# SSD decays without TensorE: broadcast rows in two buffers each, loaded a chunk ahead, and five steps of the backward states per chunk

## The chip, the cores and the metric

The kernel runs on one core of one Trainium2 chip. The metric is the device time of one execution in microseconds (us), as the median of several runs. A core has five engines that work side by side, each through its own instructions in order: TensorE (PE in the profile; PEld is its weight load), VectorE (DVE), ScalarE (ACT), GpSimd (POOL) and SyncE (SP), which here issues nearly all of the DMA transfers.

## What is computed

A two-layer backbone over 1024 latent positions and 256 context positions with 1024 features: one layer of windowed attention, then one layer with a bidirectional Mamba-2 mixer (SSD). The change lies in the second layer. Its scan is computed in chunks of 128 positions; the reference, cut to what matters here:

```python
a_cs = jnp.cumsum(da, axis=2)                      # within a chunk, per head
decay_to_end = jnp.exp(a_last[:, :, None] - a_cs)
states = jnp.einsum('bcsgn,bcsgr,bcsgrp->bcgrpn', bm, decay_to_end, xdt)
...
diff = a_cs[:, :, :, None] - a_cs[:, :, None, :]
lmat = jnp.exp(jnp.where(lower, diff, -jnp.inf))
cb = jnp.einsum('bcqgn,bcsgn->bcqsg', cm, bm)
y_diag = jnp.einsum('bcqsg,bcqsgr,bcsgrp->bcqgrp', cb, lmat, xdt)
y_off = jnp.einsum('bcqgn,bcgrpn,bcqgr->bcqgrp', cm, h_prev, jnp.exp(a_cs))
y = (y_diag + y_off)
```

This is done once forward and once on the reversed sequence, and the two results are added. There are 8 groups of 4 heads, 64 features a head, and 128 state entries.

## The kernel before, in words

The time up to about 780 us goes to the attention layer, which the change does not touch. Then `ssd_consts` (L778) computes, for all 64 rows (32 heads, two directions) and all positions, the step sizes dt, their logarithm ln, the sums acs of dt times A within each chunk (forward for rows 0 to 31, backward for 32 to 63), and from them tables with the positions on the partitions: `dtdec`, `eacs` and `dtb`, each transposed on TensorE (L885 to L889) and copied out by ScalarE (L886 to L891). Two halves of the positions go through this one after the other (L830).

The scan (`ssd`, L1025) then goes through 8 groups with 8 chunks each, 64 slots in all (`slot`, L1122). In a slot, M is a matrix of 128 x 4 x 128: for four heads, the factor between position k (partition) and position q (column). For q after k it is the forward decay times dt, otherwise the backward one, so that one M serves both directions. M times the product of B and C (`pcb`, L1130, L1134) is then the weight of four matmuls with x (L1159), which give the part of y within the chunk. L1132 and L1133 give the parts from the states before and after the chunk; L1139 and L1140 move the forward state on. The rest of a slot adds the skip term, multiplies by the gate, normalizes (L1167 to L1175) and stores the transposed result as `uN` one slot later (`tail`, L1187 to L1189).

How M comes about before the change: the sums acs and the values ln - acs are each split by `rows` (L855) into a rounded part and a remainder, and written to DRAM. For each chunk three small loads bring 20 rows into `rraw` (L1105, L1107), whose rest holds constants 0 and 1; ScalarE rounds them into `rrow` for TensorE (L1110). One matmul with `rrow` as weights and as moving operand adds a row value acs[q] and a partition value ln[k] - acs[k]. `decays` (L1114) does this for half of the heads at a time, two matmuls for the two directions (L1118), then a predicated copy takes the backward one where q is before k (L1119, mask `before`), and ScalarE applies the exponential and writes M (L1120). The first half of M for the next chunk is computed about the middle of a slot (L1166), the second half a little later (L1174).

Between these steps, `fill` lets the projections of the next group run (`front`, L911; in the last group the output projection `ssd_out`, L1261). They give TensorE most of its work: matmuls of 512 columns (L984) and 256 columns (L975, L1009), three for each product, since each operand is split into a rounded part and a remainder. Weights are loaded a use ahead (L920), rounded by ScalarE (L924) and their remainder taken by VectorE (L928).

The backward states of the next group form a chain of 11 steps (`states`, L1069): GpSimd weights x (L1059, two buffers) and decays the state before (L1064), TensorE multiplies with B into one PSUM buffer (L1082), and VectorE adds (L1094). `tick` (L1238) takes one step of this chain; a slot calls it three times at its end, as soon as the next group's x is there. What is left of the chain is issued at the end of the group (L1253).

This is the order in which the program issues instructions. A list scheduler with a model of the engines then orders them for each engine, and tile pools put in the waits where a buffer is reused. The order on each engine is thus fixed when the kernel is built. PSUM has three buffers `psX` for the small products of a slot, one `psD` and two `pj2`.

Of the kernel before, what the change touches and what calls it, by code (L numbers as in the profile page):

```python
# [9 lines left out]
F32 = mybir.dt.float32  # L10
# [3 lines left out]
ALU = mybir.AluOpType  # L14
# [30 lines left out]
    oraw=3, h1=2, h1k=8, wada=8, sqa=1,  # L45
    cacc=2, cctx=1, bT=2, cT=2, xn4=4, xn2=1, bn4=4, bn2=1, sz=2, xw=2, hf=2, hx=2, M=2, y2=1, xs=1, uT=2, pj2=2, psX=3, sk=2, dg=2,
)
# [60 lines left out]
class Kernel:  # L108
# [669 lines left out]
    def ssd_consts(self, p):  # L778
# [14 lines left out]
        self.half = t(p, [P, 1], F32, "half")  # L793
        nc.vector.memset(self.half, -0.5)
        self.eacs = t(p, [P, NCH, 64], F32, "eacs")
        self.dtdec = t(p, [P, NT, 64], F32, "dtdec")
        self.dtb = t(p, [P, NCH, 32], F32, "dtb")
        self.eal = t(p, [P, 64, NT], F32, "eal")

        self.acs_d = t(dr, [2, 64, LAT], F32, "acs")  # L800
        self.v_d = t(dr, [2, 64, LAT], F32, "vrow")
        self.before = t(p, [P, P], mybir.dt.int32, "before")
# [27 lines left out]
        for lo, n, chunks in ((0, 768, (0, 1, 2, 3, 8, 9)), (768, 512, (4, 5, 6, 7))):  # L830
# [23 lines left out]
            nc.vector.tensor_tensor_scan(out=acs[32:, ::-1], data0=keep[32:, :n][:, ::-1], data1=da[32:, ::-1], initial=0.0, op0=ALU.mult, op1=ALU.add)  # L854
            def rows(dst, src):  # L855
                h = t(q, [64, 512], F32R, "rowh", 2)
                l = t(q, [64, 512], F32R, "rowl", 2)
                nc.scalar.copy(h, src[:, :512])
                nc.vector.tensor_sub(l, src[:, :512], h)
                for x, y in enumerate((h, l)):  # L860
                    nc.sync.dma_start(dst[x, :, chunks[0] * P : chunks[0] * P + 512], y.bitcast(F32))

            rows(self.acs_d, acs)
            av = acs.rearrange("p (c n) -> p c n", n=P)
# [9 lines left out]
            nc.vector.tensor_sub(ln, ln, acs)  # L874
            rows(self.v_d, ln)

# [3 lines left out]
            nc.vector.tensor_mul(dd, dd, dt)  # L880
            nc.scalar.activation(acs, acs, AF.Exp)
            for b, c in enumerate(chunks):
                sl = slice(b * P, (b + 1) * P)
                pt = t(ps, [P, 256], F32, "psX")
                nc.tensor.transpose(pt[:, 0:64], dd[:, sl], self.ident[:64, :64])  # L885
                nc.scalar.copy(self.dtdec[:, c, :], pt[:, 0:64])  # L886
                if c < NCH:
                    nc.tensor.transpose(pt[:, 64:128], acs[:, sl], self.ident[:64, :64])
                    nc.tensor.transpose(pt[:, 128:192], dt[:, sl], self.ident[:64, :64])  # L889
                    nc.scalar.copy(self.eacs[:, c, :], pt[:, 64:128])  # L890
                    nc.scalar.copy(self.dtb[:, c, :], pt[:, 160:192])  # L891
        nc.sync.dma_start(self.eal, eal_d.broadcast_to([P, 64, NT]))

# [131 lines left out]
    def ssd(self, c0):  # L1025
# [8 lines left out]
        ps2 = self.pool("scan", ctx=c0)  # L1034


        rraw = t(ps2, [32, 6, P], F32, "rraw")
        rrow = t(ps2, [P, 6, P], F32R, "rrow")
        nc.sync.dma_start(rraw, a["rrow"].rearrange("p (r n) -> p r n", r=6))
        nc.vector.memset(rrow.bitcast(F32), 0.0)  # L1040
        ys = []
# [6 lines left out]
        def hd(d, g):  # L1048
            return slice(32 * d + 4 * g, 32 * d + 4 * g + 4)
# [19 lines left out]
        def states(g, st):  # L1069

            st["hb"] = {}
            jobs = [(0, 8), (0, 9), (1, 9), (1, 8)] + [(1, c) for c in range(NCH - 1, 0, -1)]
            xw = {}
            h = None
            for n, (d, c) in enumerate(jobs):
                if n == 0:
                    xw[0] = xweight(st, g, c, d)
                    yield
                if n + 1 < len(jobs):
                    xw[n + 1] = xweight(st, g, jobs[n + 1][1], jobs[n + 1][0])  # L1080
                s = t(ps, [P, 512], F32, "psD")[:, :256]
                nc.tensor.matmul(s, B(st, c), flat(xw.pop(n)), start=True, stop=True)  # L1082
                sv = s.rearrange("p (r h) -> p r h", r=R)
                if n in (0, 2):
                    h = t(ps2, [P, R, HP], F32, "hx")
                    nc.scalar.copy(h, sv)
                else:
                    if n == 1:
                        hn = t(ps2, [P, R, HP], F32, "hf0")
                    else:  # L1090
                        o = NCH - 1 if n == 3 else c - 1
                        hn = t(ps2, [P, R, HP], F32, f"hb{o if g % 2 == 0 else NCH - 1 - o}")
                    decay(hn, h, g, c, d)
                    nc.vector.tensor_add(hn, hn, sv)  # L1094
                    if n == 1:
                        st["hf"] = hn
                    else:
                        st["hb"][o] = h = hn
                yield

        def load_rows(n):
            g, c = divmod(n, NCH)
            cs = slice(c * P, (c + 1) * P)
            ar = self.acs_d.rearrange("h (d k) n -> (h d) k n", d=2)[:, 4 * g : 4 * g + 4, cs]
            nc.sync.dma_start(rraw[0:4, :4], ar)  # L1105
            for d in range(2):
                nc.sync.dma_start(rraw[4 + 8 * d : 12 + 8 * d, 4 + d], self.v_d[:, hd(d, g), cs])  # L1107

        def round_rows(n):
            nc.scalar.copy(rrow[:32], rraw)  # L1110
            if n + 1 < G * NCH:
                load_rows(n + 1)

        def decays(n, M, half):  # L1114

            o = t(ps, [P, 512], F32, "psX").rearrange("p (d r n) -> p d r n", d=2, r=2)
            for d in range(2):
                nc.tensor.matmul(o[:, d], rrow[:, 4 + d], rrow[:, 2 * half : 2 * half + 2], start=True, stop=True)  # L1118
            nc.vector.copy_predicated(o[:, 0], self.before.unsqueeze(1).broadcast_to([P, 2, P]), o[:, 1])  # L1119
            nc.scalar.activation(M[:, 2 * half : 2 * half + 2], o[:, 0], AF.Exp)  # L1120

        def slot(n, st, M, fill, tick, last):  # L1122

            g, c = divmod(n, NCH)
            cs = slice(c * P, (c + 1) * P)
            xc = X(st, c).rearrange("p (r h) -> p r h", r=R)
            if n + 1 < G * NCH:
                round_rows(n + 1)
            pcb = t(ps, [P, 512], F32, "psX")[:, :P]
# [5 lines left out]
            if c < NCH - 1:  # L1135
# [55 lines left out]
            self.tail = tail  # L1191
            return nM

        post = Queue()
        st = {}
        load_rows(0)
        done = 0.0
# [11 lines left out]
        for _ in chain:  # L1209
            pass  # L1210
        M = t(ps2, [P, R, P], F32, "M")
        round_rows(0)
        for half in range(2):
            decays(0, M, half)
        st["xw"] = xweight(st, 0, 0, 0)
        self.tail = None
        with ExitStack():
            for g in range(G):
# [25 lines left out]
                for c in range(NCH):  # L1244
                    def fill(x):
                        run(total * (c + sum(SEGS[: x + 1]) / sum(SEGS)) / NCH)
                    M = slot(g * NCH + c, st, M, fill, tick, g == G - 1)
                if g < G - 1:
                    run(1e9)
                    while 1 not in nst or not nst["sz"]:  # L1250
                        post.pop()
                    chain = chain or states(g + 1, nst)
                    for _ in chain:  # L1253
                        pass
                    nst["xw"] = xweight(nst, g + 1, 0, 0)
                    st = nst
# [223 lines left out]
def layout(i):  # L1480
# [26 lines left out]
    z = np.zeros((P, P), np.float32)  # L1507

    rr = np.zeros((32, 6, P), np.float32)
    for x in range(4):  # L1510
        for r in range(R):
            rr[4 + 4 * x + r, r] = 1.0
        rr[x, 4 + x % 2] = 1.0
    d["rrow"] = rr.reshape(32, -1)
    d["mask"] = np.concatenate([lm, z, rm, z, z, lm, z, z, z], 1).astype(np.float32)
# [29 lines left out]
```

## Time and profile before

| | |
|---|---|
| median of 3 runs | 1880.89 us (1879.43 to 1883.35) |
| profiled execution | 1880.79 us |
| its span, first to last instruction | 1878.7 us |
| mean granted TensorE clock | 0.980 |
| matmuls on PE | 10,632 instructions |
| DMA traffic | 192.10 MB in 147,203 packets |

Of a row that groups instructions, the name before the arrow is the tile written and those behind it are the tiles read. Three numbers with slashes are the shortest, the median and the longest duration in ns. In a row by window stand the window, its length, the busy time of each engine with its number of instructions, then the granted TensorE clock, the share of the DMA engines' time and GB/s. In a row in order of time stand start, duration, engine, line, operation and tiles; "x2" at the end means two instructions in one row, and brackets name how long the engine was idle ahead of it and whom it waited for.

### The profile page before, as it was taken

The page shows a single profiled execution, that of the slowest core. Times are in us where ns is not written, and L with a number is a line of the kernel's source. Part 1 is how long each engine was busy: PE and PEld are TensorE (multiplying, and loading weights), DVE is VectorE, ACT ScalarE, POOL GpSimd, SP SyncE. Part 2 cuts the span into 40 slices and gives each one's busy share as a digit, 9 for nine tenths or more (in the row PEclk, how much of TensorE's full clock was granted, in tenths as well). Part 3 has the DMA queues.
Part 4 walks back from the last instruction along what each step waited for, and adds up shares of the span by engine and source line. Part 5 has one row for each costly group of instructions (what it writes and reads, how often), then busy time and mean ns, then how long its engine had stood idle before and what let it go on. Part 6 is the DMA issues. An engine that isn't in the chain of part 4 may idle for free. (4 is left out here: it accounts for less than half of the span.)

```text
span 1878.7 us, 29635 instructions
## 1 busy us (share of the span) xinstructions
PE 1790.6 (95%) x10632; PEld 1541.9 (82%) x10632; DVE 1178.2 (63%) x2199; ACT 906.5 (48%) x1861; POOL 758.8 (40%) x1029
## 2 busy tenths in 40 slices
PE   6899998899999899979999999999999999999997
PEld 2687776788888786668898898989889898988887
DVE  3754426887777766584665758666575766754843
ACT  4522326677778665562353535434353544543632
POOL 4741107654456454302343343524335252442411
PEclk8899999999999999989999999999999999999998
DMA  9348756553345446111111111111111111433552
GB/s 357 108 118 260 240 167 157 126 126 95 97 120 134 113 129 222 59 56 34 38 36 44 47 33 44 39 41 36 44 47 33 47 38 39 141 117 100 177 153 78
DMA packets 147203, 192.10 MB, mean 102 GB/s; under 512 B 15312, under 2 KB 84816, under 8 KB 147056
## 3 DMA queue, kind: packets, MB, share of 16 engines
q1 hardware_dynamic: 112992, 171.56, 29.0%
q0 software_dynamic: 34064, 18.65, 5.5%
q8 instruction: 84, 1.38, 0.3%
q14 instruction: 63, 0.52, 0.1%
HBM read 154.54 MB, written 35.92 MB: 101 GB/s over the span
## 5 line engine op out<-in xcount | busy, mean ns | idle before, releaser
L229 PE MATMUL pj<-uH,wh 128*128 128x512 f32 (+1 forms) x712 | 259.3, 365 | 12.1 <-DVE v L542 2.8
L230 PE MATMUL pj<-uL,wh 128*128 128x512 f32 (+1 forms) x712 | 245.1, 345 | 1.3 <-DVE uL L298 0.9
L231 PE MATMUL pj<-uH,wl 128*128 128x512 f32 (+1 forms) x712 | 244.5, 344 | 1.1 <-POOL wl L217 1.1
L1059 POOL TENSOR_TENSOR xw<-xn,dtdec 128x256 f32<-128x256 f32 x144 | 105.9, 738 | 206.6 <-PE psD L1082 102.1
L984 PE MATMUL pj<-uH,wh 128*128 128x512 f32 x512 | 171.7, 405 | 1.1 <-ACT xn L951 1.1
L984 PE MATMUL pj<-uH,wl 128*128 128x512 f32 x512 | 171.8, 405 | 0.0
L229 PEld LDWEIGHTS pj<-uH,wh 128*128 128x128 f32 x712 | 136.7, 192 | 40.5 <-issue 11.9
L984 PE MATMUL pj<-uL,wh 128*128 128x512 f32 x512 | 168.3, 399 | 0.0
L217 POOL TENSOR_TENSOR wl<-wr,wh 128x512 fp32r<-128x512 f32 x96 | 127.2, 1329 | 77.7 <-ACT wh L215 67.1
L631 DVE TENSOR_TENSOR pl<-pt,ph 128x512 fp32r<-128x512 f32 x168 | 114.5, 687 | 64.6 <-ACT ph L630 63.5
L1009 PE MATMUL pj<-wh,uH 128*128 128x256 f32 x512 | 154.7, 302 | 0.0
L1009 PE MATMUL pj<-wh,uL 128*128 128x256 f32 x512 | 151.3, 295 | 0.0
L231 PEld LDWEIGHTS pj<-uH,wl 128*128 128x128 f32 x712 | 136.4, 192 | 17.7 <-POOL wl L217 1.5
L1009 PE MATMUL pj<-wl,uH 128*128 128x256 f32 x512 | 150.8, 295 | 0.0
L230 PEld LDWEIGHTS pj<-uL,wh 128*128 128x128 f32 x712 | 136.9, 192 | 14.0 <-DVE uL L298 1.4
L215 ACT CAST wh<-wr 128x512 fp32r<-128x512 f32 (+1 forms) x136 | 87.3, 643 | 116.8 <-PE pj L230 75.2
L1188 ACT ACTIVATE uT<-psX,nw 128x128 f32<-128x128 f32 x128 | 47.0, 367 | 189.9 <-PE psX L1187 188.8
L605 DVE CUSTOM_DVE_ANT_0 sm<-S,mask,nsink 128x640 f32<-128x640 f32 (+2 forms) x160 | 119.1, 772 | 26.7 <-PE S L602 13.8
L630 ACT CAST ph<-pt 128x512 fp32r<-128x512 f32 x168 | 97.6, 586 | 61.8 <-PE pt L626 56.2
L607 ACT ACTIVATE sm<-sm,nm 128x640 f32<-128x640 f32 (+2 forms) x160 | 118.5, 742 | 9.5 <-DVE nm L605 9.0
L1154 POOL TENSOR_TENSOR xs<-xn,sk 128x256 f32<-128x256 f32 x64 | 42.0, 657 | 184.8 <-DVE sk L1150 183.6
L984 PEld LDWEIGHTS pj<-uL,wh 128*128 128x128 f32 x512 | 95.6, 188 | 19.9
(330 smaller groups left out, 4990.5 us busy)
## 6 DMA issues: line engine op xcount, KB each, us to landing
wr<-w_x SPq DMA_DIRECT2D x32, 512.0 KB
wr<-wo SPq DMA_DIRECT2D x48, 256.0 KB
wr<-w_sk SPq DMA_DIRECT2D x24, 512.0 KB
wr<-wg SPq DMA_DIRECT2D x40, 256.0 KB
qs<-q POOLq DMA_DIRECT2D x40, 256.0 KB, 4.0
wada<-w_ada SPq DMA_DIRECT2D x16, 512.0 KB
wr<-wq SPq DMA_DIRECT2D x32, 256.0 KB
wl<-w_ada SPq DMA_DIRECT2D x32, 256.0 KB
```

Source lines behind the costliest of these rows:

```text
L215: nc.scalar.copy(h, raw)
L217: (eng or nc.vector).tensor_tensor(l, raw, h, op=ALU.subtract)
L229: self.nc.tensor.matmul(ps, lh, rh, start=first and i == 0, stop=False)
L230: self.nc.tensor.matmul(ps, lh, rl, start=False, stop=False)
L231: self.nc.tensor.matmul(ps, ll, rh, start=False, stop=last and i == n - 1)
L605: nc.vector.tensor_tensor_reduce(out=sm[:, :W], in0=Sv, in1=self.mask[:, m0 : m0 + W], scale=-SCALE, scalar=self.nsink[:, 4 * j + r : 4 * ...
L607: nc.scalar.activation(sm[:, :W], sm[:, :W], AF.Exp, bias=nm[:, r : r + 1], scale=-1.0, accum_out=sums[:, r : r + 1])
L630: nc.scalar.copy(ph, ptf)
L631: nc.vector.tensor_sub(pl, ptf, ph)
L984: nc.tensor.matmul(raw[:, 512 * i : 512 * i + 512], l[:, k, :], r[i][:, k, :], start=k + y == 0, stop=k == KT - 1 and y == 2)
L1009: nc.tensor.matmul(pj[:, c], l, r[:, k, :], start=c % 2 + q + k + y == 0, stop=c % 2 == 1 and q == 1 and k == 3 and y == 2)
L1059: nc.gpsimd.tensor_tensor(xw, X(st, c).rearrange("p (r h) -> p r h", r=R), self.dtdec[:, c, hd(d, g)].unsqueeze(2).broadcast_to([P, R, HP] ...
```

## The change

M is no longer formed by matmuls. The sums acs are written to DRAM once, unrounded. For each chunk, two loads copy four rows of them to all 128 partitions: the forward rows straight into the tile of M, the backward rows into a tile `bw` (`load_rows`). Each has two buffers. The forward rows for slot n + 2 are asked for in slot n behind the four matmuls that read M, and the backward ones at the start of slot n. GpSimd then adds to the backward rows a value per partition and head, `vd` (`offset`), the predicated copy takes them into M for both halves at once, now from SBUF (`merge`), and ScalarE applies the exponential head by head with a bias per partition, `vf` (`decays`). `vf` is ln - acs of the forward direction, and `vd` that of the backward direction less `vf`; both tables come from one more transposition for each of the 8 chunks in `ssd_consts`. The exponential of acs there goes to a tile of its own, as acs is still needed.

Further, a slot calls `tick` five times, after `fill(0)` and `fill(1)` as well; and the weighted x for a group's first chunk is taken in the last step of the chain of the backward states instead of after it. The constants `rrow` are gone.

```diff
-        self.acs_d = t(dr, [2, 64, LAT], F32, "acs")
-        self.v_d = t(dr, [2, 64, LAT], F32, "vrow")
+        self.vf = t(p, [P, NCH, 32], F32, "vf")
+        self.vd = t(p, [P, NCH, 32], F32, "vd")
+        self.acs_d = t(dr, [64, LAT], F32, "acs")
...
-            rows(self.acs_d, acs)
+            nc.sync.dma_start(self.acs_d[:, chunks[0] * P : chunks[0] * P + 512], acs[:, :512])
...
-            rows(self.v_d, ln)
-            nc.scalar.activation(acs, acs, AF.Exp)
+            ea = t(q, [64, n], F32, "ea")
+            nc.scalar.activation(ea, acs, AF.Exp)
...
+                    nc.tensor.transpose(pt[:, 192:256], ln[:, sl], self.ident[:64, :64])
+                    nc.scalar.copy(self.vf[:, c, :], pt[:, 192:224])
+                    nc.vector.tensor_sub(self.vd[:, c, :], pt[:, 224:256], self.vf[:, c, :])
...
                 if n + 1 < len(jobs):
                     xw[n + 1] = xweight(st, g, jobs[n + 1][1], jobs[n + 1][0])
+                else:
+                    st["xw"] = xweight(st, g, 0, 0)
...
-        def load_rows(n):
-            g, c = divmod(n, NCH)
-            cs = slice(c * P, (c + 1) * P)
-            ar = self.acs_d.rearrange("h (d k) n -> (h d) k n", d=2)[:, 4 * g : 4 * g + 4, cs]
-            nc.sync.dma_start(rraw[0:4, :4], ar)
-            for d in range(2):
-                nc.sync.dma_start(rraw[4 + 8 * d : 12 + 8 * d, 4 + d], self.v_d[:, hd(d, g), cs])
-        def round_rows(n):
-            nc.scalar.copy(rrow[:32], rraw)
-            if n + 1 < G * NCH:
-                load_rows(n + 1)
+        def load_rows(n, d, tag):
+            g, c = divmod(n, NCH)
+            x = t(ps2, [P, R, P], F32, tag)
+            nc.sync.dma_start(x, self.acs_d[hd(d, g), c * P : (c + 1) * P].unsqueeze(0).broadcast_to([P, R, P]))
+            return x
+        def offset(n, bw):
+            g, c = divmod(n, NCH)
+            nc.gpsimd.tensor_tensor(bw, bw, self.vd[:, c, 4 * g : 4 * g + 4].unsqueeze(2).broadcast_to([P, R, P]), op=ALU.add)
+        def merge(M, bw):
+            nc.vector.copy_predicated(M, self.before.unsqueeze(1).broadcast_to([P, R, P]), bw)
         def decays(n, M, half):
-            o = t(ps, [P, 512], F32, "psX").rearrange("p (d r n) -> p d r n", d=2, r=2)
-            for d in range(2):
-                nc.tensor.matmul(o[:, d], rrow[:, 4 + d], rrow[:, 2 * half : 2 * half + 2], start=True, stop=True)
-            nc.vector.copy_predicated(o[:, 0], self.before.unsqueeze(1).broadcast_to([P, 2, P]), o[:, 1])
-            nc.scalar.activation(M[:, 2 * half : 2 * half + 2], o[:, 0], AF.Exp)
+            g, c = divmod(n, NCH)
+            for r in range(2 * half, 2 * half + 2):
+                nc.scalar.activation(M[:, r], M[:, r], AF.Exp, bias=self.vf[:, c, 4 * g + r : 4 * g + r + 1])
...
             if n + 1 < G * NCH:
-                round_rows(n + 1)
+                offset(n + 1, bw[n + 1])
+            if n + 2 < G * NCH:
+                bw[n + 2] = load_rows(n + 2, 1, "bw")
...
             fill(0)
+            tick()
...
             fill(1)
-            nM = None
+            tick()
+            if n + 2 < G * NCH:
+                fw[n + 2] = load_rows(n + 2, 0, "M")
             if n + 1 < G * NCH:
-                nM = t(ps2, [P, R, P], F32, "M")
-                decays(n + 1, nM, 0)
+                merge(fw[n + 1], bw.pop(n + 1))
+                decays(n + 1, fw[n + 1], 0)
...
             fill(2)
-            if nM is not None:
-                decays(n + 1, nM, 1)
+            if n + 1 < G * NCH:
+                decays(n + 1, fw[n + 1], 1)
```

More of the change, by code (lines that the diff above doesn't have):

```diff
@@ L45 @@
     oraw=3, h1=2, h1k=8, wada=8, sqa=1,
-    cacc=2, cctx=1, bT=2, cT=2, xn4=4, xn2=1, bn4=4, bn2=1, sz=2, xw=2, hf=2, hx=2, M=2, y2=1, xs=1, uT=2, pj2=2, psX=3, sk=2, dg=2,
+    cacc=2, cctx=1, bT=2, cT=2, xn4=4, xn2=1, bn4=4, bn2=1, sz=2, xw=2, hf=2, hx=2, M=2, bw=2, y2=1, xs=1, uT=2, pj2=2, psX=3, sk=2, dg=2,
 )
@@ L854, in ssd_consts @@
             nc.vector.tensor_tensor_scan(out=acs[32:, ::-1], data0=keep[32:, :n][:, ::-1], data1=da[32:, ::-1], initial=0.0, op0=ALU.mult, op1=ALU.add)
[L855 to L861, printed above, removed]
-            rows(self.acs_d, acs)
+            nc.sync.dma_start(self.acs_d[:, chunks[0] * P : chunks[0] * P + 512], acs[:, :512])
             av = acs.rearrange("p (c n) -> p c n", n=P)
@@ L887, in ssd_consts @@
                 if c < NCH:
-                    nc.tensor.transpose(pt[:, 64:128], acs[:, sl], self.ident[:64, :64])
+                    nc.tensor.transpose(pt[:, 64:128], ea[:, sl], self.ident[:64, :64])
                     nc.tensor.transpose(pt[:, 128:192], dt[:, sl], self.ident[:64, :64])
@@ L1034, in ssd @@
         ps2 = self.pool("scan", ctx=c0)
[L1037 to L1040, printed above, removed]
         ys = []
@@ L1099, in states, with slot @@
                 yield
-        def load_rows(n):
+        def load_rows(n, d, tag):
             g, c = divmod(n, NCH)
-            cs = slice(c * P, (c + 1) * P)
-            ar = self.acs_d.rearrange("h (d k) n -> (h d) k n", d=2)[:, 4 * g : 4 * g + 4, cs]
-            nc.sync.dma_start(rraw[0:4, :4], ar)
-            for d in range(2):
-                nc.sync.dma_start(rraw[4 + 8 * d : 12 + 8 * d, 4 + d], self.v_d[:, hd(d, g), cs])
-        def round_rows(n):
-            nc.scalar.copy(rrow[:32], rraw)
-            if n + 1 < G * NCH:
-                load_rows(n + 1)
-        def decays(n, M, half):
-            o = t(ps, [P, 512], F32, "psX").rearrange("p (d r n) -> p d r n", d=2, r=2)
-            for d in range(2):
[L1118 to L1122, printed above, removed]
-            g, c = divmod(n, NCH)
+            x = t(ps2, [P, R, P], F32, tag)
[6 more added lines that the diff above has]
+            nc.vector.copy_predicated(M, self.before.unsqueeze(1).broadcast_to([P, R, P]), bw)
+        def decays(n, M, half):
+            g, c = divmod(n, NCH)
+            for r in range(2 * half, 2 * half + 2):
+                nc.scalar.activation(M[:, r], M[:, r], AF.Exp, bias=self.vf[:, c, 4 * g + r : 4 * g + r + 1])
+        def slot(n, st, fill, tick, last):
+            g, c = divmod(n, NCH)
+            M = fw.pop(n)
             cs = slice(c * P, (c + 1) * P)
@@ L1191, in slot @@
             self.tail = tail
-            return nM
         post = Queue()
         st = {}
-        load_rows(0)
+        fw, bw = [{n: load_rows(n, d, tag) for n in range(2)} for d, tag in enumerate(("M", "bw"))]
+        offset(0, bw[0])
+        merge(fw[0], bw.pop(0))
         done = 0.0
@@ L1210, in ssd @@
             pass
-        M = t(ps2, [P, R, P], F32, "M")
-        round_rows(0)
         for half in range(2):
-            decays(0, M, half)
-        st["xw"] = xweight(st, 0, 0, 0)
+            decays(0, fw[0], half)
         self.tail = None
@@ L1246, in fill @@
                         run(total * (c + sum(SEGS[: x + 1]) / sum(SEGS)) / NCH)
-                    M = slot(g * NCH + c, st, M, fill, tick, g == G - 1)
+                    slot(g * NCH + c, st, fill, tick, g == G - 1)
                 if g < G - 1:
@@ L1254, in ssd @@
                         pass
-                    nst["xw"] = xweight(nst, g + 1, 0, 0)
                     st = nst
@@ L1507, in layout @@
     z = np.zeros((P, P), np.float32)
[L1509 to L1514, printed above, removed]
     d["mask"] = np.concatenate([lm, z, rm, z, z, lm, z, z, z], 1).astype(np.float32)
```

## The prediction

> **What bounds the kernel now.** I read the page first, for the engines' shares. Then I cut the span into its stages with the busy times by window, and last I read TensorE in order of time inside the stage that the change touches.
>
> ```profile
> PE 1790.6 (95%) x10632; PEld 1541.9 (82%) x10632; DVE 1178.2 (63%) x2199; ACT 906.5 (48%) x1861; POOL 758.8 (40%) x1029
> ```
>
> ```profile
> core 0: us, PE busy (x) PEld busy (x) DVE busy (x) ACT busy (x) POOL busy (x), PEclk, DMA share, GB/s
> 814.00:836.00 22.00, 11.84 (x67) 9.88 (x66) 20.39 (x28) 17.34 (x47) 0.00 (x0) 0.69 0.24 75
> ...
> 965.00:1073.50 108.50, 108.02 (x684) 97.56 (x684) 71.07 (x132) 47.58 (x98) 43.68 (x67) 1.00 0.14 41
> 1073.50:1617.00 543.50, 540.65 (x3413) 488.18 (x3412) 356.27 (x658) 238.70 (x487) 219.41 (x332) 1.00 0.15 46
> 1617.00:1795.00 178.00, 176.06 (x953) 151.41 (x954) 110.78 (x190) 81.03 (x158) 71.41 (x91) 1.00 0.42 128
> ```
>
> The scan loop fills the last three of these windows and part of the time before. One group of eight chunks takes 108.5 us (965 to 1073.5, then five more in 543.5 us), so a chunk takes 13.6 us. PE is busy 108.02 of 108.50 us at a granted clock of 1.00, while DVE has 71, ACT 48 and POOL 44 us of work. A busy PE is not yet a full PE, since a matmul's modelled duration overlaps the next, so I looked at the starts:
>
> ```profile
> 1001.12 0.28 PE L1009 MATMUL pj<-wh,uL 128*128 128x256 f32 x1
> 1001.24 0.40 PE L1118 MATMUL psX<-rrow 128*128 128x256 f32 x2
> 1001.47 0.40 PE L984 MATMUL pj<-uH,wh 128*128 128x512 f32 x1
> 1001.71 0.59 PE L1082 MATMUL psD<-xw,bn 128*128 128x256 f32 x2
> ```
>
> ```profile
> 1038.76 0.40 PE L1118 MATMUL psX<-rrow 128*128 128x256 f32 x2
> 1039.00 0.39 PE L984 MATMUL pj<-uH,wl 128*128 128x512 f32 x1
> ```
>
> Starts follow each other at 0.12 us for 256 columns and 0.24 us for 512, with nothing between. The stage is bound by TensorE's order of instructions, one behind the other, and the only wait that recurs is one at each group's start:
>
> ```profile
> 964.99 0.28 PE L1187 MATMUL psX<-ident,y 128*128 128x128 f32 x1
> 965.75 0.70 PE L1082 MATMUL psD<-xw,bn 128*128 128x256 f32 x2 [0.48 <-POOL xw L1059]
> ```
>
> **What goes from TensorE.** The decays took two matmuls for each half chunk (L1118).
>
> ```profile
> L1118 PE MATMUL psX<-rrow x256: 276/281/365, 832.2 to 1769.4; 128*128 128x256 f32 x128
> L1119 DVE COPY_PREDICATED psX<-before,psX x128: 408/422/430, 833.3 to 1772.6; 128x256 f32<-128x256 int32 x128
> L1120 ACT ACTIVATE M<-psX x128: 357/368/392, 834.5 to 1773.1; 128x256 f32<-128x256 f32 x128
> L1110 ACT CAST rrow<-rraw x64: 814/826/836, 829.9 to 1752.4; 32x768 fp32r<-32x768 f32 x64
> ```
>
> Their price is not the 281 ns of the row but what they keep the next matmul from starting: 1001.47 less 1001.24 for two, 0.115 us each, and 0.12 at 1038.76. I take 0.1175: 256 x 0.1175 = **30.1 us**, all on the path, as PE waits for nobody around them. Eight transposes of 64 columns come in, in a stretch where PE waits anyway (below). The order of instructions of the changed kernel has just these 248 matmuls fewer on PE.
>
> **What the other engines get, per chunk.** *DVE* loses two predicated copies, 2 x 0.422 = 0.84 us, and gets one of 128x512 from SBUF. The trace has none, so I bound it by 0.42 (half its size, above) and 1.24 (twice its size, two SBUF inputs, L928 below). I take 0.69, the DVE row of the same size among L217's. Net -0.15 us. One merge for both halves now stands ahead of all four exponentials; M is needed only after the next chunk's first product, so the later first half costs nothing.
>
> ```profile
> L217 POOL TENSOR_TENSOR wl<-wr,wh x96: 1263/1295/1804, 33.1 to 765.6; 128x512 fp32r<-128x512 f32 x96
> L217 DVE TENSOR_TENSOR wl<-wr,wh x40: 672/693/1226, 130.4 to 1852.7; 128x512 fp32r<-128x512 f32 x32, 128x1024 fp32r<-128x1024 f32 x8
> ```
>
> *ACT* loses the rounding (0.83) and two exponentials (0.74) and gets four of 128x128 with a bias per partition. They lie between 0.19, a copy of 32 columns (L891, below), and 0.37, the same shape read from PSUM with a scale per partition (L1188). I take 0.37: 1.48 against 1.57, net -0.1.
>
> ```profile
> L1188 ACT ACTIVATE uT<-psX,nw x128: 347/368/392, 925.4 to 1791.9; 128x128 f32<-128x128 f32 x128
> ```
>
> *POOL* gets one addition of 128x512. Between 1.22 (two of its 128x256 at 0.61, L1059 below) and 1.80 (L217's longest) I take 1.30: 64 x 1.30 = 83 us, 10.4 in a group, so 44 becomes 54 of some 104 us. None of the three becomes the bound on average; the gain of DVE and ACT is off the path and counts as nothing.
>
> *SP and DMA.* Three small loads a chunk become two of 256 KB, 33.6 MB in 128 loads.
>
> ```profile
> q1 hardware_dynamic: 112992, 171.56, 29.0%
> ...
> qs<-q POOLq DMA_DIRECT2D x40, 256.0 KB, 4.0
> ...
> rraw<-vrow SPq DMA_DIRECT2D x128, 4.0 KB
> ```
>
> By bytes they cost 33.6/171.56 of 29.0% of the span, 107 us of all 16 engines. By packets of 512 B (65,536) at the queue's mean of 77 ns (29.0% x 16 x 1878.7 / 112992) it is 315 us. So the DMA share of 0.15 in the loop becomes 0.27 to 0.5, and 0.5 to 0.8 beside the output weights after 1617. A load of 256 KB landed 4.0 us after its issue. The forward rows are asked for when the chunk's last use of their buffer (L1159) is over and merged a chunk, some 13 us, later; the backward rows have as long. Price: nothing, with 9 us of cover. Behind a waiting M load on SP stand the next uN store and weight load; those weights too are fetched at least one use ahead.
>
> **The start of the stage.** From 814 to 836 us PE has 11.84 of 22 us of work and waits for the decay sums.
>
> ```profile
> 817.77 0.62 ACT L858 CAST rowh<-w 64x512 fp32r<-64x512 f32 x1 [1.66 <-DVE w L854]
> 818.40 1.28 ACT L869 ACT_TABLE_LOAD   x1
> 819.70 0.21 ACT L869 ACTIVATE et<-tot 64x4 f32<-64x4 f32 x1
> 819.81 0.60 ACT L858 CAST rowh<-w 64x512 fp32r<-64x512 f32 x1
> ```
>
> ```profile
> 822.71 0.37 PE L888 MATMUL psX<-ident,w 64*128 64x64 f32 x1 [6.89 <-ACT dtdec L886]
> ```
>
> ```profile
> 823.33 0.19 ACT L891 COPY dtb<-psX 128x32 f32<-128x32 f32 x1
> ```
>
> Four such roundings (2.4 us on ACT) go ahead of that wait. Eight copies of 0.19 (1.5 us) and eight transposes come in behind it. A third round between ACT and PE for each set of three PSUM buffers is new. I put this at 0, with 3 us either way.
>
> **Five steps of the backward states per chunk.** Two more ticks let the chain of the next group run denser. On the path stand only the 0.48 us waits at the group starts: at best 7 x 0.48 = 3.4 us go. I count 0, because POOL, which they wait for, gets busier. The weighted x for a group's first chunk (L1255) moves from the group's end into the last step of that chain: the same one instruction of 0.61 us on POOL, earlier.
>
> **The sum.** The profiled execution took 1880.8 us (span 1878.7), the median of the three runs is 1880.9, so its own time serves. 1880.8 - 30.1 + 0 + 0 = 1850.7, **1851 us**.
>
> **Rivals.** *1. POOL becomes the pace where the backward states run, and the kernel gets slower.* Each of the 11 steps of a group needs a weighted x (L1059) and a decayed state (L1064) from POOL before PE may go on.
>
> ```profile
> 965.00:1010.20 45.20, 44.72 (x320) 42.16 (x320) 27.61 (x56) 17.61 (x40) 26.00 (x41) 1.00 0.16 49
> ```
>
> ```profile
> L1059 POOL TENSOR_TENSOR xw<-xn,dtdec x144: 609/615/1617, 864.3 to 1728.1; 128x256 f32<-128x256 f32 x144
> ```
>
> ```profile
> L1064 POOL TENSOR_TENSOR hf<-hf,eal 128x256 f32<-128x256 f32 x48 | 29.9, 623 | 0.0
> ```
>
> ```profile
>   POOL xw L1059: 9.0, 16
> ```
>
> The last row is all that PE waited for POOL at L1082: 9.0 us, 16 times. In that stretch POOL is 58% busy (26.00 of 45.20). In the changed order the fullest chunk has 16 POOL instructions between two rows of ss, two of them the new addition, where it had 12: 14 x 0.62 + 2 x 1.30 = 11.3 of some 13.1 us. If each of 7 x 11 = 77 steps then waits as the first does now, 77 x 0.48 = 37 us come back: 1851 + 37 = **1888**, 7 us slower than before. It decides above 30.1/77 = 0.39 us a step. Against it: the steps now run with one wait in eleven. For it: how that one wait arises.
>
> ```profile
> 963.91 1.32 DVE L928 TENSOR_TENSOR wl<-wr,wh 128x1024 fp32r<-128x1024 f32 x1
> 964.11 1.59 POOL L1059 TENSOR_TENSOR xw<-xn,dtdec 128x256 f32<-128x256 f32 x1
> ```
>
> POOL's instruction takes 1.59 us in place of 0.61, and ends about 0.5 us after a DVE instruction with two SBUF inputs that started just ahead of it. The new addition and the new merge both read two SBUF operands, so such meetings become more frequent: with half of the 0.48 at each step, 18 us come back and the time is **1869**. The Trainium skill ("SBUF — State Buffer", section "SBUF: two separate sides") states this as a rule against the change: GpSimd and a DVE instruction with two SBUF inputs take a shared pair of ports in turns, each for a whole instruction. By that rule the two rows above are one case of it, which the trace bears out.
>
> *2. The freed time is not given back.* If DVE were the real bound, removing matmuls would only make PE wait and the time would stay at **1881**. For it: some stretches in which DVE is full.
>
> ```profile
> 1055.50:1064.50 9.00, 9.00 (x49) 7.73 (x49) 8.97 (x16) 3.42 (x6) 4.41 (x6) 1.00 0.24 74
> ```
>
> Against it: over a group DVE has 71 of 108.5 us, the work taken away is DVE's as well, and PE's starts have no gaps. The same time would come out if the removed matmuls stood in gaps; the two quoted pairs do not.
>
> *3. The broadcast loads come late.* Should one land over 13 us after its issue, merge, exponentials and the product M wait, and behind them the four L1159 on PE with everything after them. It is likeliest in the last group, beside the output weights: 8 chunks x 1 to 2 us, **1859 to 1867**. The 4.0 us of the 256 KB row speak against it.
>
> **How the numbers follow.** Forecast, 1843 to 1857: 0.63. POOL's waits in part, 1857 to 1876: 0.20. Rival 1 in full, 1888: 0.07. Rival 2: 0.05. Rival 3: 0.03. Below 1843: 0.02. The low end is 1851 - 3 (start) - 3.4 (group starts), 1844, less one for the price of a matmul: 1843. The high end takes in half a wait per step, 1869. About 2 in 10 are left out. A measurement of this kernel can tell 0.2% (3.8 us) from no change. Faster by more than that: 0.88; within: 0.05; slower: 0.07.
>
> **What would show it.** Right: no L1118, group periods of about 104.7 us (108.5 - 32 x 0.1175), starts on PE still 0.12 and 0.24 us apart, POOL's addition near 1.3 us, the merge near 0.7, an exponential at or below 0.37. Rival 1: PE idle for POOL far above 9 us, more POOL rows of 1 us and over, a group period of 105 to 110 us. Rival 2: PE idle for DVE. Rival 3: DVE waiting for a DMA on M ahead of the merge. Wrong altogether: a loop whose PE is as gapless as now and not some 30 us shorter.

## The result and the profile after

The changed kernel takes 1960.99 us (median of 4 runs, 1959.29 to 1967.76) beside 1882.12 us for the kernel before on the same chip (4 runs, 1879.43 to 1885.53). The ratio is 1.0429 with a 95% interval of 1.0406 to 1.0452: 79 us slower, and 110 us over the forecast. The profiled execution has a span of 1957.6 us at a mean granted clock of 0.969.

The page of the changed kernel, engines first, then the DMA queue, two costly groups and the issues of the two loads:

```profile
PE 1801.2 (92%) x10384; PEld 1529.4 (78%) x10384; DVE 1172.3 (60%) x2138; ACT 885.4 (45%) x1929; POOL 827.5 (42%) x1093
...
q1 hardware_dynamic: 177488, 203.19, 35.0%
...
L1102 POOL TENSOR_TENSOR bw<-bw,vd 128x512 f32<-128x512 f32 x64 | 67.3, 1052 | 322.9 <-DMA bw<-acs 316.5
...
L1112 ACT ACTIVATE M<-M,vf 128x128 f32<-128x128 f32 x256 | 82.6, 391 | 160.8 <-DVE M L1106 156.7
...
M<-acs SPq DMA_DIRECT2D x64, 256.0 KB, 5.0
bw<-acs SPq DMA_DIRECT2D x64, 256.0 KB, 5.0
```

The 248 matmuls are gone, and no engine got much more work: POOL has 69 us more, DVE 6 and ACT 21 us less. Yet the span grew, so the time is idle time and, as the granted clock shows, some slower running. It lies in every group. Busy times by window of the changed kernel, from one group's end to the next (before: 108.02 of 108.50 us at a clock of 1.00):

```profile
1006.00:1125.50 119.50, 110.00 (x650) 96.15 (x649) 70.20 (x123) 44.86 (x105) 52.67 (x76) 0.97 0.27 71
1125.50:1244.00 118.50, 109.92 (x652) 96.63 (x650) 70.21 (x123) 45.17 (x105) 52.33 (x75) 0.97 0.29 72
1244.00:1718.00 474.00, 436.04 (x2587) 382.14 (x2588) 284.08 (x496) 180.85 (x422) 209.28 (x294) 0.97 0.30 80
```

A group takes 118.5 us. PE is idle for 8.6 of them, and its granted clock is 0.97. What PE waits for between 880 and 1800 us, the three largest rows (us in total, times, longest):

```profile
PE psD L1074 <- DVE hb L1086: 18.9, 8, 3.9
PE psX L1127 <- DVE y L1165: 16.3, 16, 2.9
PE psD L944 <- DVE cctx L905: 16.1, 8, 3.1
```

PE waits mostly for DVE (and, at L1074, its weight load waits for POOL's `xw` as well, 19.1 us in 6 times). But DVE has 70 us of work in 118.5 and POOL 53, so the question is what these two stand for themselves. Who waits for whom, over the whole execution of the changed kernel (us in total, times, longest):

```profile
POOL bw L1102 <- DMA bw<-acs: 316.5, 61, 63.6
...
DVE y L1165 <- POOL y L1152: 118.1, 45, 7.0
...
DVE M L1106 <- DMA M<-acs: 88.6, 33, 5.6
```

One of the 61 waits, 63.6 us, lies ahead of the scan and is there in every kernel below that keeps these loads, the fastest too. The other 60 are 252.9 us, 4.2 each. POOL stands ahead of nearly every addition to the backward rows until their load has landed; DVE stands ahead of every second merge in the same way, and then stands again for the y that POOL adds. The order of time shows how. Rows of the changed kernel on SP, DVE and POOL, most others left out:

```profile
1145.38 0.36 SPq L1097 DMA_DIRECT2D M<-acs  x1
...
1150.22 0.74 DVE L1106 COPY_PREDICATED M<-before,bw 128x512 f32<-128x512 int32 x1 [5.25 <-DMA M<-acs]
1151.03 0.36 SPq L1097 DMA_DIRECT2D bw<-acs  x1
...
1155.57 1.04 POOL L1102 TENSOR_TENSOR bw<-bw,vd 128x512 f32<-128x512 f32 x1 [3.22 <-DMA bw<-acs]
1156.57 0.73 POOL L1152 TENSOR_TENSOR y<-y,xs 128x256 f32<-128x256 f32 x1
1157.34 0.42 DVE L1165 TENSOR_TENSOR y<-y,psX 128x256 f32<-128x256 f32 x1 [1.33 <-POOL y L1152]
1157.67 0.68 DVE L1129 TENSOR_TENSOR M<-M,psX 128x512 f32<-128x512 f32 x1
...
1166.42 0.73 DVE L1106 COPY_PREDICATED M<-before,bw 128x512 f32<-128x512 int32 x1
...
1181.63 0.75 DVE L1106 COPY_PREDICATED M<-before,bw 128x512 f32<-128x512 int32 x1 [2.53 <-DMA M<-acs]
```

The merge at 1150.22 is the next chunk's. It stands ahead of the multiplication of this chunk's own M with `pcb` (1157.67), though its M is multiplied only one chunk later. It frees a `bw` buffer, and the load at 1151.03 goes into it. The addition to those rows starts at 1155.57, as soon as they are there; their merge is the second after, at 1181.63. So the addition had 26 us to spare, and yet POOL held up the y sum (L1152) for it, and DVE's L1165 and L1129 behind that. On an engine that works in order, the place of an instruction decides, not the time by which its result is needed.

### The profile page after: what moved, and what is told of

It reads as the page before. It is cut to its first block, busy times and chain, and to the rows that moved or that the text cites. A ratio compares the mean times of both kernels' runs of the same rounds, so it can differ in the third digit from the quotient of the medians.

```text
span 1957.6 us, 29146 instructions
## 1 busy us (share of the span) xinstructions
PE 1801.2 (92%) x10384; PEld 1529.4 (78%) x10384; DVE 1172.3 (60%) x2138; ACT 885.4 (45%) x1929; POOL 827.5 (42%) x1093
## 5 line engine op out<-in xcount | busy, mean ns | idle before, releaser
L1102 POOL TENSOR_TENSOR bw<-bw,vd 128x512 f32<-128x512 f32 x64 | 67.3, 1052 | 322.9 <-DMA bw<-acs 316.5
L980 PE MATMUL pj<-uH,wl 128*128 128x512 f32 x512 | 165.5, 401 | 0.0
L1005 PE MATMUL pj<-wh,uL 128*128 128x256 f32 x512 | 156.0, 305 | 0.0
L1112 ACT ACTIVATE M<-M,vf 128x128 f32<-128x128 f32 x256 | 82.6, 391 | 160.8 <-DVE M L1106 156.7
L231 PEld LDWEIGHTS pj<-uH,wl 128*128 128x128 f32 x712 | 137.2, 193 | 19.3 <-POOL wl L217 3.2
L230 PEld LDWEIGHTS pj<-uL,wh 128*128 128x128 f32 x712 | 138.0, 194 | 14.2 <-DVE uL L298 1.5
L1049 POOL TENSOR_TENSOR xw<-xn,dtdec 128x256 f32<-128x256 f32 x144 | 98.9, 693 | 78.0 <-PE psD L1074 58.3
L607 ACT ACTIVATE sm<-sm,nm 128x640 f32<-128x640 f32 (+2 forms) x160 | 118.5, 742 | 9.5 <-DVE nm L605 9.1
L980 PEld LDWEIGHTS pj<-uH,wl 128*128 128x128 f32 x512 | 96.2, 189 | 21.2
```

What stands on the lines that cost most here:

```text
L230: self.nc.tensor.matmul(ps, lh, rl, start=False, stop=False)
L231: self.nc.tensor.matmul(ps, ll, rh, start=False, stop=last and i == n - 1)
L607: nc.scalar.activation(sm[:, :W], sm[:, :W], AF.Exp, bias=nm[:, r : r + 1], scale=-1.0, accum_out=sums[:, r : r + 1])
L980: nc.tensor.matmul(raw[:, 512 * i : 512 * i + 512], l[:, k, :], r[i][:, k, :], start=k + y == 0, stop=k == KT - 1 and y == 2)
L1005: nc.tensor.matmul(pj[:, c], l, r[:, k, :], start=c % 2 + q + k + y == 0, stop=c % 2 == 1 and q == 1 and k == 3 and y == 2)
L1049: nc.gpsimd.tensor_tensor(xw, X(st, c).rearrange("p (r h) -> p r h", r=R), self.dtdec[:, c, hd(d, g)].unsqueeze(2).broadcast_to([P, R, HP] ...
```

## The experiments

The theory: the order of instructions puts POOL's addition and DVE's merge so close behind their load that these engines stand until it has landed, with everything else queued behind them; nothing else of the change costs much. (That the scheduler does so because its model has the load landed by then, as the expectations say, no run shows.) The rivals: POOL has too much work (Rival 1 of the prediction), the five steps crowd it, or the traffic of the loads slows the rest. Experiments 1, 2, 3 and 7 are single runs; the others were timed in rounds against the kernel before. Experiments 1 to 4 ran on one chip and 5 to 8 on another; the kernel before took 1881.15 us on the first and 1881.54 on the second.

**1. Three steps in place of five.** `slot` without the two new ticks:

```diff
             fill(0)
-            tick()
...
             fill(1)
-            tick()
```

> Undoes one part: three steps of the backward states per slot, as before, with all else as in the changed kernel. Theory (the built order puts GpSimd's addition and VectorE's merge right where its model has a load landed; the load takes 5 us on the chip, and the engine stands with all that is queued behind): the additions still wait about 5 us each for the DMA, 1945 to 1965 us. Rival, the denser steps overload GpSimd: at least half of the 110 us over my forecast goes, 1850 to 1905.

Measured: 1976.12 us, slower than with five. The waits between 880 and 1800 us:

```profile
POOL bw L1102 <- DMA bw<-acs: 264.1, 55, 8.9
...
DVE M L1106 <- DMA M<-acs: 80.1, 37, 5.3
...
PE psX L1134 <- POOL xw L1049: 25.5, 4, 7.0
```

The waits for the loads are much like those of the changed kernel. The rival on the steps falls; the time lies 11 us above what the theory allowed, so with these waits the five steps are worth some 15 us, by one run. The last row names a place for it: four times PE waits for the weighted x of a group's first chunk, which is taken in the last step of the chain of backward states; that it comes late because three steps leave more of the chain to the group's end is argued, not shown. The changed kernel's profile has next to nothing there.

**2. No loads of the backward rows.** The addition keeps its size, but takes a constant in place of the loaded rows, so M lacks the backward sums:

```diff
+            if d:
+                return x
...
-            nc.gpsimd.tensor_tensor(bw, bw, self.vd[:, c, 4 * g : 4 * g + 4].unsqueeze(2).broadcast_to([P, R, P]), op=ALU.add)
+            nc.gpsimd.tensor_tensor(bw, low.unsqueeze(2).broadcast_to([P, R, P]), self.vd[:, c, 4 * g : 4 * g + 4].unsqueeze(2).broadcast_to([P, R, P]), op=ALU.add)
```

> Leaves out the 64 loads of the backward sums: GpSimd's addition, of the same size, takes a constant for them, so the backward decays are not those of the reference. The loads into M stay. Theory: the 316 us of waits for the DMA on GpSimd are gone, the waits of the merge for M (89 us before) stay; 1865 to 1910. Rival, the addition itself costs the time (GpSimd full, or its ports shared with VectorE): no change, 1945 to 1965.

Measured: 1903.08 us, 58 us less, with the same 64 additions on POOL. What stays are waits for the forward rows (880 to 1800 us):

```profile
POOL bw L1107 <- DVE M L1111: 181.0, 58, 8.6
...
DVE M L1111 <- DMA M<-acs: 156.8, 60, 5.6
```

At least these 58 us are not the price of POOL's work but of its wait for the load. With that wait gone the merge waits for its own load in nearly every chunk, and POOL for the merge, whose buffer it refills.

**3. The addition held behind the y sum.** Same loads, same buffers; only the place of the addition in POOL's order is tied down, by an edge that lets it be issued after L1152:

```diff
-            if n + 1 < G * NCH:
-                offset(n + 1, bw[n + 1])
...
-            nc.gpsimd.tensor_tensor(yv, yv, xs, op=ALU.add)
+            add = nc.gpsimd.tensor_tensor(yv, yv, xs, op=ALU.add)
+            if n + 1 < G * NCH:
+                with self.tc.issue_after(add.ins):
+                    offset(n + 1, bw[n + 1])
```

> Nothing left out: GpSimd's addition for slot n + 1 is made to stand behind the last addition to y of slot n on GpSimd; the merge stays where the planner puts it. Theory: additions wait under 20 us in all, what stays is the merge's wait for M, 1865 to 1910. Rival, the DMA traffic itself delays everything: no change, 1945 to 1965. Rival, lead too short: waits for the DMA stay, 1930 or more.

Measured: 1862.32 us, 99 us less than the changed kernel and just below the expected range. Of POOL's waits for these loads, in the whole execution, the one ahead of the scan is left, and the merge now waits for the addition instead:

```profile
POOL bw L1102 <- DMA bw<-acs: 64.0, 1, 64.0
...
DVE M L1106 <- POOL bw L1102: 26.4, 15, 4.1
```

Here the theory was wrong in one part. It expected the merge's wait for M's load to stay; DVE no longer waits for a load of M at all, though the merge was not tied down.

**4. The merge held too,** behind the multiplication by the gate:

```diff
+            nc.vector.tensor_add(yv, yv, yd[:, :256].rearrange("p (r h) -> p r h", r=R))
+            mul = nc.vector.tensor_mul(yf, yf, st["sz"][c])
             if n + 1 < G * NCH:
-                merge(fw[n + 1], bw.pop(n + 1))
+                with self.tc.issue_after(mul.ins):
+                    merge(fw[n + 1], bw.pop(n + 1))
                 decays(n + 1, fw[n + 1], 0)
-            nc.vector.tensor_add(yv, yv, yd[:, :256].rearrange("p (r h) -> p r h", r=R))
-            nc.vector.tensor_mul(yf, yf, st["sz"][c])
```

> As the run before, and the merge into M for slot n + 1 is made to stand behind the product with the gate in slot n on VectorE, so that a chunk lies between a load and its use. Theory: neither engine waits for these loads any more (under 20 us in all) and the removed matmuls show, 1848 to 1866, faster than before. Rivals (GpSimd overloaded, traffic): 1900 or more.

Measured: 1858.15 us (4 runs, 1854.97 to 1863.76) beside 1881.15 for the kernel before; ratio 0.988, interval 0.9856 to 0.9903. By window:

```profile
969.00:1074.50 105.50, 104.97 (x656) 94.00 (x655) 73.10 (x126) 45.50 (x108) 55.63 (x79) 1.00 0.29 82
1074.50:1180.00 105.50, 104.75 (x652) 93.75 (x650) 71.15 (x124) 45.38 (x106) 54.01 (x75) 1.00 0.31 81
1180.00:1600.00 420.00, 417.29 (x2589) 373.57 (x2588) 282.70 (x491) 179.61 (x417) 215.24 (x295) 1.00 0.32 87
```

The group takes 105.5 us, with PE full, the clock at 1.00, POOL's 54 us of work and a DMA share of 0.29 to 0.32. The loads themselves, from the row of their line in this kernel:

```profile
DMA to landing us min/median/max: 4.4/5.1/8.1
```

They land as late as in the changed kernel (4.4/5.0/8.0 there), and in the loop neither POOL nor DVE waits for them. That rules out traffic, POOL's load and the landing time as such. What costs is where the wait stands. Beside these groups, one of the changed kernel is 13 us longer: PE has 8.6 us of idle time instead of 0.5 to 0.75, and a clock of 0.97 instead of 1.00 makes some 3.5 us by estimate (0.03 x 118.5), 11 to 12 in all.

**5. The five steps alone in the kernel before.** Two more ticks and the weighted x inside the chain; the decays stay on TensorE:

```diff
+                else:
+                    st["xw"] = xweight(st, g, 0, 0)
...
             fill(0)
+            tick()
...
             fill(1)
+            tick()
```

> The kernel before with one part of the change alone: two more steps of the backward states per chunk (five in place of three), and the weighted x of a group's first chunk inside that chain. Decays stay on TensorE. Theory (no loads of M or bw, so nothing to stand for): at most the 0.48 us waits at seven group starts go, 3.4 us, so 1877 to 1884, the same within what can be measured. Rival (the five steps themselves crowd GpSimd and make TensorE wait): 1890 or more, and TensorE waits for xw or hf well above 9 us.

Measured: 1885.91 us (10 runs) beside 1881.54; ratio 1.0033, interval 1.0021 to 1.0045. A loss of some 4 us, just above the expected range. The waits of PE for POOL did shrink, as the theory had it (between 880 and 1800 us, 3.4 us in 7 waits before):

```profile
PE psD L1084 <- POOL xw L1059: 1.4, 2, 1.0
```

So the loss is not a wait for POOL. One part can be named in the profiled execution, a slow stretch of TensorE's clock behind a wait near the end (last section), worth some 1.5 us by estimate (16 matmuls 0.21 us apart in place of 0.12). Where the rest lies was not found out.

**6. Both held, three steps.** Experiment 4 without the two new ticks.

> The changed kernel with both the addition and the merge held behind the y sums of the chunk, but three steps of the backward states per chunk as before. Theory: once nothing stands waiting for a load, the number of steps is worth little, 1855 to 1866 beside 1858 with five. Rival (the five steps are worth in every state the 15 us that they were worth in the changed kernel as it stands): 1870 to 1876.

Measured: 1854.65 us (4 runs, 1851.82 to 1859.41); ratio 0.9866, interval 0.9844 to 0.9888. It is the fastest kernel here, but its interval overlaps that of experiment 4, so three and five steps are not told apart. The 15 us of experiment 1 were seen only where the engines stand for loads.

**7. Only the merge held;** the addition stays where it was. The edit is that of experiment 4 without that of experiment 3.

> The changed kernel with only the merge held behind the multiplication by sz; the addition stays where it is. Theory: GpSimd's additions still stand for the loads of bw, some 60 times at 4 to 6 us (250 to 320 us in all), while VectorE's wait for M's load is gone: 1925 to 1960. Rival (the merge's place on VectorE is what costs): 1855 to 1875, with GpSimd's waits harmless.

Measured: 1889.24 us, and the theory's size misses by 36 us. The waits came as foretold (whole execution; 205.5 us in 52 without the first):

```profile
POOL bw L1102 <- DMA bw<-acs: 269.2, 53, 63.7
PE psD L1074 <- POOL xw L1049: 10.6, 8, 1.7
```

They cost only 31 us over experiment 4, where merge and addition together cost 103. Experiment 3 does not price the merge's wait, since that wait went with the addition's; experiment 2, where the merge waits for M and POOL for the merge, lies 45 us over experiment 4. So the waits of the two engines are not two sums to be added. In the changed kernel they stand in one chain: a load of M, the merge that waits for it, the load of `bw` into the buffer which that merge frees, the addition that waits for this one, then the y sum and the multiplication that PE needs. Rows of the changed kernel:

```profile
1175.39 0.36 SPq L1097 DMA_DIRECT2D M<-acs  x1
...
1182.44 0.36 SPq L1097 DMA_DIRECT2D bw<-acs  x1
...
1187.26 1.04 POOL L1102 TENSOR_TENSOR bw<-bw,vd 128x512 f32<-128x512 f32 x1 [2.90 <-DMA bw<-acs]
...
1190.87 0.42 DVE L1165 TENSOR_TENSOR y<-y,psX 128x256 f32<-128x256 f32 x1 [4.48 <-POOL y L1152]
```

With the merge at 1181.63 (above) between the first two, that is 15.5 us from a load to a sum on DVE, with two landings in it. Holding either end breaks this chain: in experiment 7 DVE waits for no load of M, in experiment 3 neither engine waits for a load in the loop. That the chain makes up the whole difference between 31 and 103 us is argued, not shown.

**8. Both held, and the new tables late.** The eight transposes for `vf` and `vd` moved behind all others of the start:

```diff
-                    nc.tensor.transpose(pt[:, 192:256], ln[:, sl], self.ident[:64, :64])
...
+            lns.append((ln, chunks))
+        for ln, chunks in lns:
...
+                    nc.tensor.transpose(pt[:, 0:64], ln[:, b * P : (b + 1) * P], self.ident[:64, :64])
```

> The changed kernel with both held, and the eight transposes that make vf and vd moved behind all other transposes of the start of the stage. Theory: the start, some 2.6 to 4.7 us later than before because each of the new round trips stands ahead of the next transposes, gets 2 to 4 us of it back: 1853 to 1857 beside 1858. Rival (the start waits for something else, for instance for the first loads of bw and M): 1858, within 1 us.

Measured: 1858.52 us (4 runs); ratio 0.9889, interval 0.987 to 0.9908, the same as experiment 4. Other waits come in place of those taken away: PE in this kernel, at the first projections behind the tables:

```profile
842.69 1.12 PE L950 MATMUL pj<-ident,cacc 128*128 128x128 f32 x4 [8.56 <-ACT xn L953]
```

The theory for this one falls: the order of the start is not improved by this move. The equal times hide two differences. The first multiplication of M starts at 903.73 us beside 896.65 in experiment 4, but a group takes 104.8 us beside 105.5. The edit is outside the loop, but the scheduler has ordered the loop anew as well: behind the third group's first multiplication of M, POOL's next two instructions write `xs` and `xw` in experiment 4, `xw` and `hf` here. Why this order is the shorter one was not looked into. Every experiment was scheduled anew like this, so differences of a few us between two of them need not come from the edit alone.

## Why the prediction was wrong

**The step that failed** is the price of the loads, "Price: nothing, with 9 us of cover". The 9 us came from 13 us between load and use as the program is written, less 4.0 us of landing. The landing was 5.0 us, which would have mattered little. The 13 us are what did not hold, though not because the result was needed earlier: the rows loaded at 1151.03 are merged at 1181.63. The order of instructions on each engine is fixed when the kernel is built. In it the addition's turn on POOL came at 1152.35 (1155.57 - 3.22), 1.3 us after its load was issued, and the merge's turn on DVE at 1144.97 (1150.22 - 5.25), 0.4 us before its own. Both stood until the load had landed, ahead of work that is needed at once. The prediction took the time between load and need for cover; cover is the time between a load and the place of the first instruction that waits for it in its engine's order. It used the built order for TensorE, and for POOL to count instructions, but not to see where addition and merge stand behind their loads. Of the 110 us missed, experiment 4 gives back 103 by tying down these two instructions.

**Rival 3** (loads late) was the nearest, but had the wrong place (DVE, in the last group), the wrong condition (a landing over 13 us) and a price of 1859 to 1867. POOL's wait, which it did not name, is three times DVE's.

**Rival 2** (DVE the real bound) has its sign without its cause: PE is idle for DVE in the changed kernel. But in experiment 4 DVE has as much work in a group (71 to 73 us beside 70), and between 880 and 1800 us PE waits for it once, 1.1 us.

**TensorE's 30.1 us** were right in mechanism and nearly in size: a group takes 105.5 us in experiment 4 and 104.8 in experiment 8, against 104.7 foretold and 108.5 before. Of the whole 30.1 us, experiment 4 shows 23.0 and experiment 6 shows 26.9 against the kernel before. PE is still idle for 0.5 to 0.75 us of a group in experiment 4. It is 7 us above 1851; if all eight groups are 0.8 us longer than foretold, an estimate, that is 6.4 of it.

**The engines' work.** POOL's addition took 1.04 us (1.30 taken) and 67 us in all (83). The four exponentials of a chunk take 1.29 us (82.6 us in 64 chunks; 1.48 taken): one lasts 0.39 us, a little more than the 0.37 foretold, but they overlap. The merge is the 0.7 us that were taken; the line's row in the changed kernel:

```profile
L1106 DVE COPY_PREDICATED M<-before,bw x64: 721/742/1554, 839.9 to 1814.1; 128x512 f32<-128x512 int32 x64
```

The DMA share of the loop, 0.27 to 0.30, lies in the range given. So **Rival 1** does not hold, in full or in part, though it had the kernel slower and POOL in its way: its reason was POOL's work, and POOL stood for loads instead; with as much work on POOL in experiment 4, no wait of PE for POOL is left between 880 and 1800 us.

**The start of the stage** was put at 0, 3 us either way. In the kernel before:

```profile
815.41 0.40 PE L885 MATMUL psX<-ident,w 64*128 64x64 f32 x3 [0.78 <-DVE w L880]
...
865.00 1.12 PE L1082 MATMUL psD<-xw,bn 128*128 128x256 f32 x2 [0.31 <-POOL xw L1059]
```

and in the changed one:

```profile
817.97 0.58 PE L878 MATMUL psX<-ident,w 64*128 64x64 f32 x3 [2.55 <-DVE w L872]
...
867.58 0.70 PE L1074 MATMUL psD<-xw,bn 128*128 128x256 f32 x2 [0.31 <-POOL xw L1049]
```

From the end of PE's work ahead of the wait to the first backward state it is 865.00 - (815.41 - 0.78) = 50.4 us before and 52.2 us after: 1.8 us longer, inside the 3 us.

**The five steps** were put at 0, with 3.4 us as the best. Alone they cost 4.4 us (experiment 5), so the sign was wrong by a size that is just measurable, though of the 3.4 us of waits only 1.4 were left.

## What to carry to other kernels

A load is hidden if the first instruction that waits for it stands late enough in the order of its engine; when the result is needed says nothing about that. So after moving loads, look in the built order, on every engine, for the distance between each load and its first waiting instruction, and for what is queued behind that. If a scheduler places it too early, an ordering edge behind the current chunk's work is enough: here two such edges turned 1961 us into 1858, with the same work and the same traffic, and the one on the addition alone gave 1862 in a single run. The waits that a profile adds up for one engine are not the price of their cause: POOL's 205 us of waits cost 31 in experiment 7, and went together with DVE's in experiment 3.

## What was not expected of the hardware

*Short waits cost clock too.* Two stretches by window of the changed kernel, the wait and what follows it:

```profile
1124.00:1128.00 4.00, 1.64 (x14) 1.44 (x13) 0.68 (x3) 0.59 (x1) 3.85 (x7) 1.00 0.13 39
1128.00:1132.00 4.00, 3.79 (x17) 3.70 (x18) 2.90 (x5) 2.44 (x8) 2.70 (x3) 0.57 0.10 28
...
1244.00:1248.00 4.00, 1.36 (x10) 1.34 (x11) 2.26 (x5) 0.57 (x3) 3.50 (x6) 1.00 0.11 17
1248.00:1252.00 4.00, 4.00 (x22) 3.95 (x21) 1.34 (x2) 1.87 (x6) 1.48 (x2) 0.57 0.26 52
```

and PE in order of time at the first:

```profile
1125.24 0.28 PE L1005 MATMUL pj<-wh,uH 128*128 128x256 f32 x1
1125.36 0.28 PE L1005 MATMUL pj<-wl,uH 128*128 128x256 f32 x1
1128.21 0.88 PE L1074 MATMUL psD<-xw,bn 128*128 128x256 f32 x2 [2.57 <-DVE hb L1086]
...
1129.32 0.41 PE L1005 MATMUL pj<-wl,uH 128*128 128x256 f32 x1
1129.53 0.41 PE L1005 MATMUL pj<-wh,uL 128*128 128x256 f32 x1
```

After 2.57 us of idle time the same matmul of 256 columns starts every 0.21 us in place of 0.12, for some 3.7 us. A clock of 0.57 for 4 us is 1.7 us on top of a wait of 2.6. Over the windows from 1006 to 1718 us the mean of 0.97 makes this 0.03 x 712 = 21 us in six groups, by estimate. In that stretch the clock falls only near waits of 2.6 to 3.9 us, or near two of about 1 us in a row. The length of the wait does not decide alone. Waits of 2.23 and 2.27 us at 1095 and 1331 us left the clock at 1.00, and near the end of the kernel before and of experiment 5 PE has the same wait of 1.92 us. What follows it in the kernel before:

```profile
1830.00:1834.00 4.00, 4.00 (x36) 4.00 (x35) 0.00 (x0) 0.00 (x0) 1.02 (x2) 1.00 0.63 199
```

and in experiment 5:

```profile
1830.00:1834.00 4.00, 3.54 (x22) 3.57 (x23) 1.84 (x3) 0.81 (x2) 2.15 (x2) 0.74 0.96 313
```

The wait ends at 1828.35 us in the first and at 1830.46 in the second; only in the second do matmuls then start 0.21 us apart, for 3.4 us. What decides was not found out. The Trainium skill ("TensorE: Matmul & The Clock Gate", section "What's actually happening") has the clock halved after an idle window of about 3.4 us. The trace agrees on a rate of about half; the waits that were followed by it here were mostly shorter.

*A load of rows copied to all partitions landed later than most loads of its size.* 256 KB in pieces of 512 B landed 5.0 us after issue at the median, 4.4 at best and 8.0 at worst. The prediction took 4.0 from a load of 256 KB that GpSimd issues; 256 KB of weights issued by SP landed in 2.8 us (`wo`) and 3.7 us (`wg`) in the changed kernel. Whether the copying is the reason was not tested.
